# First values drained before the first normalising multiplications, two buffers for the first squares, and k prepared ahead of q

## The chip, the cores and the metric

The kernel runs on one core of one Trainium2 chip. The metric is the device time of one execution in microseconds; the median over several runs counts. Lower is better.

## The reference

A two-layer causal decoder trunk over 512 tokens of width 1024, in float32. Layer 0 has two kinds of attention heads side by side (8 dilated heads "A", 8 sliding-window heads "B" with sinks that share two k/v heads); layer 1 has 16 "forgetting" heads "C". Each layer ends with a squared-ReLU MLP of width 4096.

```python
def forgetting_attention(q, k, v, log_f):         # layer 1; A and B differ in bias and mask
    c = jnp.cumsum(log_f, axis=1)
    s = jnp.einsum("bqhd,bshd->bhqs", qb, k) * scale + c_q - c_k       # causal mask
    return jnp.einsum("bhqs,bshd->bqhd", softmax(s), v)

def reference(x, g_mix, g_mlp, ...):
    for layer in range(2):
        h = rms_norm(x, g_mix[layer])
        # mixer: q, k, v = h @ w_in; q, k = rms_norm per head; attention; @ w_out
        x = x + mixer(h, ...)
        h = rms_norm(x, g_mlp[layer])
        x = x + jnp.square(jax.nn.relu(h @ w_up[layer])) @ w_down[layer]
    return x
```

## The kernel before, in words

Every float32 matrix product is made of three products of rounded parts: an operand x is split into a high part (`whi`, `h[:,0]`, written by ACT or POOL as a cast) and a low part (`wlo`, the remainder, a subtraction on DVE or POOL), and hi·hi + lo·hi + hi·lo are summed in a PSUM bank. So nearly every weight tile needs two elementwise passes before TensorE (PE) may use it.

The work of the five engines is written as one Python program. A scheduling layer then records an order for each engine by its own estimates of durations; instructions passed to `in_order` (while `cnt["start"]` is set) or to `tc.keep_in_program_order` keep the written order among themselves. On the chip each engine works through its recorded order and waits at semaphores. Nearly all transfers are on the queue of SP.

The start of layer 0 runs so:

1. `start` loads the transposed input and the first weights and projects q and k of the first four A heads into the four PSUM banks `pj0` to `pj3` (one for each tile of 128 tokens; L663). Mask tables are built meanwhile on DVE in scratch tiles, of which `f` has the tag `P3` with two buffers.
2. The next projection, `v_a(0)`, makes the first values v into four other banks (L234 to L236, 128x256 matmuls); the one behind it, `kv_b`, makes k and v of the B heads and takes the banks of `v_a(0)` again, each once that is drained.
3. `norm_heads` (L243) copies the q/k banks to the SBUF tiles `qk` (L250), squares them on ACT into a tile with the tag `sq`, of which layer 0 has one buffer (L254), reduces the squares over each head on DVE (L255), takes the inverse root in a chain of small DVE steps (L265 to L268, `rsqrt_small` L130 to L135, in the tile `room`), and multiplies `qk` by it: token tiles 0 and 2 on DVE, 1 and 3 on POOL (L274, `NORM = 'vgvg'`). At the first use the same chain also yields `rcol`, the inverse root mean square of each token (L276).
4. `prep_v` (L310) drains the value banks: for each bank an ACT scaling by `rcol` (L160) and a DVE subtraction (L161), which frees the bank.
5. For each pair of heads, `get` makes the transposed operands. `prep_q` transposes q with four PE transposes (L283, `qkT`), then two ACT casts (L293) and two DVE subtractions (L294). `prep_k` transposes k likewise, then for each of its two heads an ACT scaling (L160), a DVE subtraction (L161) and a transfer on SP that copies k to the other 64 partitions (L306, `K<-K`). Scores (`S`, L341) of a head need its K with that transfer, and its half of Q.

`attend` runs the heads (scores, softmax with P scaled by POOL, DVE or ACT at L363 and L366, transposes of P, L378, values, L398, drained to `yf` at L402), and `run` interleaves them with dense projections (`pj`) or the output projection (`op`).

Of the kernel before, what the change touches and what calls it, by code (L numbers as in the profile page):

```python
# [18 lines left out]
P = 128  # L19
# [3 lines left out]
NT = S // P  # L23
FF = 4096
HD = 64
# [12 lines left out]
NORM = 'vgvg'  # L38
# [31 lines left out]
def trunk(ctx, tc, x, b_sinks, w_out_even, b_forget, w_out_odd, w_up, w_down, xt, gains, w_in_even, w_in_odd, out):  # L70
    nc = tc.nc
# [9 lines left out]
    def bank(tag, name):  # L81
        return ps.tile([P, 512], F32, tag=tag, bufs=BANKS[tag], name=name)
# [114 lines left out]
    def layer_attention(li, hT, w_in, w_out, stats=None):  # L197


        with ExitStack() as c2:  # L200
# [42 lines left out]
            def norm_heads(outs, nh, sq_tag="sq", sq_bufs=1 + li, ms=None):  # L243


                w = nh * HD
                qk = [ap.tile([P, 2, 512], F32, tag="qk", bufs=4, name="qk") for _ in range(2)]
                ss = small.tile([P, NT, 8], F32, tag="ss", name="ss")
                for t in range(NT):
                    nc.scalar.copy(qk[t // 2][:, t % 2, :w], outs[t][:, :w])  # L250
                for t in range(NT):
                    q = qk[t // 2][:, t % 2, :w]
                    sq = ap.tile([P, 512], F32, tag=sq_tag, bufs=sq_bufs, name="sq")
                    nc.scalar.activation(sq[:, :w], q, AF.Square)  # L254
                    nc.vector.reduce_sum(ss[:, t, :nh], sq[:, :w].rearrange("p (h d) -> p h d", d=HD), axis=AX.X)  # L255
                if ms is None:
                    v = small.tile([P, NT, 8], F32, tag="ssv", name="ssv")[:, :, :nh]
                    rs = small.tile([P, NT, 8], F32, tag="rs", name="rs")[:, :, :nh]
                    room = None
                else:  # L260
                    room = ap.tile([P, 512], F32, tag=sq_tag, bufs=sq_bufs, name="room")
                    room = [room[:, i * NT * (nh + 1):(i + 1) * NT * (nh + 1)]
                            .rearrange("p (t h) -> p t h", h=nh + 1) for i in range(5)]
                    v, rs = room[:2]
                    nc.vector.tensor_scalar(v[:, :, nh], ms, 1.0 / D, EPS, op0=OP.mult, op1=OP.add)  # L265
                    nc.vector.tensor_scalar_mul(ecol, v[:, :, nh], EPS)
                for t in range(NT):
                    nc.vector.tensor_scalar(v[:, t, :nh], ss[:, t, :nh], 1.0 / HD, ecol[:, t:t + 1],  # L268
                                            op0=OP.mult, op1=OP.add)
                rsqrt_small(rs, v, room)  # L270
                for t in range(NT):
                    q = qk[t // 2][:, t % 2, :w].rearrange("p (h d) -> p h d", d=HD)
                    eng = nc.gpsimd if NORM[t] == "g" else nc.vector
                    eng.tensor_mul(q, q, rs[:, t, :nh].unsqueeze(2).to_broadcast([P, nh, HD]))  # L274
                if ms is not None:
                    nc.vector.tensor_copy(rcol, rs[:, :, nh])  # L276
                return qk

            def head_T(qk, off):
# [229 lines left out]
            st = {}  # L509

            def v_use(g, i):
                def use(outs):
                    st["v", g] = prep_v(outs, 0, 4, i)
                return use

            def qk_use(key, nh, *sq):
# [8 lines left out]
            if li == 0:  # L525
                def qk_a(g):
                    return project([(g * 768, g * 768 + 512)], qk_use(g, 8))

                def v_a(g):
                    return project([(g * 768 + 512, g * 768 + 768)], v_use(g, 0), PAT_START if g == 0 else PAT_ATT)  # L530

                def att_a(g):
                    def get(p_):
                        qk = st["qk", g]
                        return prep_q(qk, p_ * P), prep_k(qk, 256 + p_ * P, gg[:, 0:1])
                    return attend(get, 256, lambda: st["v", g], lambda j: j, "a", 4 * g, 2, 2 * g)

                def kv_b():
                    def use(outs):
                        st["v", 3] = prep_v(outs, P, 2, 1)  # L540
                        st["k", "b"] = norm_heads(outs, 2)
                    return project([(2048, 2304)], use, PAT_START)

                def att_b():
                    def get(p_):
                        if p_ == 0:
                            st["kb"] = prep_k(st["k", "b"], 0, gg[:, 1:2])
                        k = st["kb"][p_ // 2]
                        return prep_q(st["qk", "b"], p_ * P), [k, k]
                    return attend(get, 0, lambda: st["v", 3], lambda j: j // 4, "b", 0, 4, 4)  # L550

                start(ap, hT, w_in, make_tables(ap, dist, lt, lb), [bank("pA", f"pj{t}") for t in range(NT)], qk_use(0, 8))
                all_of(v_a(0))
                run(att_a(0), 32, chain(kv_b(), project([(1536, 2048)], qk_use("b", 8))), 768, LEADS[0])
                run(att_b(), NB, chain(qk_a(1), v_a(1)), 768, LEADS[1])
                run(chain(att_a(1), last_values()), 38, chain(out_part([0, 1, 4, 5], True),
                                                              out_part([6, 7], False), ahead([2, 3])), 1536, LEADS[2])
                last = [2, 3]
            else:
                def qk_c(g):  # L560
                    return project([(g * 768, g * 768 + 512)], qk_use(g, 8))

                def v_c(g):
                    return project([(g * 768 + 512, g * 768 + 768)], v_use(g, g))

                def vf_c():
                    def use(outs):
                        forget(ap, outs)
                        v_use(0, 0)(outs)
                    return project([(512, 768), (3072, 3088)], use, PAT_START)  # L570

                def att_c(g):
                    def get(p_):
                        qk = st["qk", g]
                        return prep_q(qk, p_ * P), prep_k(qk, 256 + p_ * P, gg[:, 2:3])
                    return attend(get, 256, lambda: st["v", g], lambda j: j, "c", 4 * g, 2, 2 * g)

                g = vf_c()
                for _ in range(STATS):
                    next(g)  # L580
                stats()
                all_of(g)
                all_of(qk_c(0))
                for g in range(3):
                    run(att_c(g), 36, chain(qk_c(g + 1), v_c(g + 1)), 768, LEADS[3 + g])
                run(chain(att_c(3), last_values()), 42, chain(out_part([0, 1, 2, 3], True),
                                                              out_part([4, 5], False), ahead([6, 7])), 1536, LEADS[6])
                last = [6, 7]
# [683 lines left out]
```

## Time and profile before

| what | us |
|---|---|
| median of 3 runs | 1165.46 (1165.13 to 1166.15) |
| profiled execution, its own time | 1166.66 |
| its span | 1164.9 |
| PE busy with matmuls | 1145.0 (98% of the span) |
| DVE busy | 875.5 (75%) |
| ACT busy | 645.9 (55%) |
| POOL busy | 200.3 (17%) |

A line of a timeline reads: start in us, duration in us, engine, source line, operation, output<-input, shape, count; in brackets the idle time of the engine ahead of it and what ended that. PE is TensorE, DVE VectorE, ACT ScalarE, POOL GpSimd, SPq the transfer queue of SP. A line of stretches reads: from:to, length, and for PE, its weight loads, DVE, ACT and POOL the busy time with the number of instructions, then the granted clock of PE, the share of the DMA engines in use, and GB/s. Some matmul records can be missing from a trace.

### The profile page before, as it was taken

How to read it: one execution, taken by the hardware profiler on the slowest of the kernel's cores; microseconds unless marked ns; L12 is line 12 of the kernel's file. 1: busy time of each engine (PE TensorE's matmuls, PEld its weight loads, DVE VectorE, ACT ScalarE, POOL GpSimd, SP SyncE). 2: the span in 40 equal slices, each digit the busy share in tenths (PEclk: the TensorE clock that was granted, in tenths of full speed). 3: DMA queues.
4: the chain of work that ended last, by engine and by line, in shares of the span. 5: the costliest groups of instructions: out<-in, count | busy, mean ns of one | idle time of the engine just before them, and what ended most of it. 6: DMA issues, size and time to landing. Idle time of an engine off the chain costs nothing.

```text
span 1164.9 us, 17364 instructions
## 1 busy us (share of the span) xinstructions
PE 1145.0 (98%) x6228; PEld 980.3 (84%) x6228; DVE 875.5 (75%) x1865; ACT 645.9 (55%) x1342; POOL 200.3 (17%) x292
## 2 busy tenths in 40 slices
PE   9899999999999999999999999999999999999998
PEld 7887887888988988988887888888888888888887
DVE  7787899968967847855646877778858759669676
ACT  7365867565545545444335685656756455465452
POOL 0345434200000000000155445342100000000000
PEclk9899999999999999999999999999999999999999
DMA  8423115242332332333443333343430721623403
GB/s 287 129 75 91 37 37 148 71 127 73 102 116 91 91 109 91 93 118 106 149 122 121 106 86 109 95 133 112 164 104 4 234 90 56 197 73 109 148 34 109
DMA packets 94695, 126.57 MB, mean 109 GB/s; under 512 B 5888, under 2 KB 66304, under 8 KB 94608
## 3 DMA queue, kind: packets, MB, share of 16 engines
q1 hardware_dynamic: 93568, 123.29, 34.7%
q10 hardware_dynamic: 1040, 2.16, 0.5%
q8 instruction: 49, 0.80, 0.3%
q14 instruction: 38, 0.31, 0.1%
HBM read 114.39 MB, written 4.23 MB: 102 GB/s over the span
## 4 chain that ended last, share of the span: by engine, by line
PE 84%; DVE 7%; DMA 3%; ACT 3%; issue 2%; POOL 2%; SPq 0%; POOLq 0%; ACTq 0%; DVEq 0%
PE up L165 10%; PE up L168 10%; PE up L169 10%; PE pj L236 4%; PE pj L234 4%; PE pj L235 4%; PE O L398 3%; PE PT L378 2%; PE op L169 2%; PE op L165 2%; PE op L168 2%; PE Y L1032 2%; PE Y L1030 2%; PE Y L1033 2%; PE S L341 2%
## 5 line engine op out<-in xcount | busy, mean ns | idle before, releaser
L165 PE MATMUL up<-xin,whi 128*128 128x512 f32 x512 | 200.5, 392 | 0.0
L169 PE MATMUL up<-xin,whi 128*128 128x512 f32 x512 | 199.3, 389 | 0.0
L168 PE MATMUL up<-xin,wlo 128*128 128x512 f32 x512 | 199.2, 389 | 0.0
L779 ACT CAST whi<-wraw 128x512 fp32r<-128x512 f32 x228 | 139.2, 619 | 105.1 <-PE up L169 47.4
L780 DVE TENSOR_TENSOR wlo<-wraw,whi 128x512 fp32r<-128x512 f32 x228 | 151.6, 685 | 50.9 <-ACT whi L779 50.8
L169 PEld LDWEIGHTS up<-xin,whi 128*128 128x128 f32 x512 | 96.1, 188 | 20.2
L165 PEld LDWEIGHTS up<-xin,whi 128*128 128x128 f32 x512 | 96.1, 188 | 19.8 <-issue 0.2
L168 PEld LDWEIGHTS up<-xin,wlo 128*128 128x128 f32 x512 | 96.2, 188 | 19.6 <-issue 0.2
L358 ACT ACTIVATE P<-P,negm 128x128 f32<-128x128 f32 (+5 forms) x128 | 69.4, 543 | 46.5 <-DVE negm L355 44.6
L153 POOL TENSOR_SCALAR whi<-wraw 128x512 fp32r<-128x512 f32 x88 | 60.1, 684 | 167.3 <-PE pj L236 123.6
L961 ACT ACTIVATE u<-up 128x512 f32<-128x512 f32 x64 | 38.3, 599 | 90.9 <-PE up L169 90.9
L234 PE MATMUL pj<-whi,hn 128*128 128x512 f32 (+2 forms) x256 | 88.7, 347 | 0.0
L236 PE MATMUL pj<-whi,hn 128*128 128x512 f32 (+2 forms) x256 | 86.9, 340 | 0.0
L235 PE MATMUL pj<-wlo,hn 128*128 128x512 f32 (+2 forms) x256 | 86.8, 339 | 0.0
L800 DVE TENSOR_TENSOR t<-u 128x256 f32<-128x256 f32 x56 | 23.1, 423 | 62.9 <-ACT u L1104 61.1
L156 POOL TENSOR_TENSOR wlo<-wraw,whi 128x512 fp32r<-128x512 f32 x48 | 64.0, 1335 | 21.0 <-ACT whi L151 18.6
L366 POOL TENSOR_SCALAR P<-P,rden 128x256 f32<-128x256 f32 (+2 forms) x96 | 48.9, 512 | 81.5 <-DVE rden L361 76.0
L156 DVE TENSOR_TENSOR wlo<-wraw,whi 128x512 fp32r<-128x512 f32 (+1 forms) x71 | 48.2, 685 | 18.5 <-POOL whi L153 15.0
L390 ACT CAST PT<-PT 128x256 fp32r<-128x256 f32 (+3 forms) x128 | 49.1, 403 | 21.5 <-PE PT L378 20.6
L234 PE MATMUL pj<-whi,h 128*128 128x256 f32 (+1 forms) x160 | 55.4, 346 | 4.6 <-DVE v L161 4.1
L355 DVE CUSTOM_DVE_ANT_0 P<-S,bias 128x128 f32<-128x128 f32 (+1 forms) x96 | 45.7, 485 | 17.8 <-PE S L344 11.9
L779 ACT CAST whi<-mraw 128x512 fp32r<-128x512 f32 x64 | 38.8, 619 | 33.1 <-DVE mraw L890 14.4
(241 smaller groups left out, 3092.1 us busy)
## 6 DMA issues: line engine op xcount, KB each, us to landing
wraw<-in_w_up SPq DMA_DIRECT2D x64, 512.0 KB, 4.3
wraw<-in_w_down SPq DMA_DIRECT2D x56, 512.0 KB, 3.8
wraw<-in_w_in_odd SPq DMA_DIRECT2D x22, 512.0 KB, 3.8
wraw<-in_w_in_even SPq DMA_DIRECT2D x17, 512.0 KB, 4.7
mraw<-in_w_down SPq DMA_DIRECT2D x16, 512.0 KB, 4.7
K<-K SPq DMA_DIRECT2D x26, 256.0 KB, 2.9
bias<-csp SPq DMA_DIRECT2D x16, 256.0 KB, 3.3
wraw<-in_w_out_odd SPq DMA_DIRECT2D x8, 512.0 KB, 3.8
```

What stands on the lines that cost most here:

```text
L153: nc.gpsimd.tensor_scalar(dst_h, src, 1.0, 1.0, op0=OP.mult, op1=OP.mult)
L156: in_order((nc.gpsimd if lo == "pool" else nc.vector).tensor_sub(dst_l, src, dst_h.bitcast(F32)))
L165: m = nc.tensor.matmul(o, wh, xh, start=start, stop=False, skip_group_check=more)
L168: nc.tensor.matmul(o, wl, xh, start=False, stop=False, skip_group_check=more)
L169: nc.tensor.matmul(o, wh, xl, start=False, stop=stop, skip_group_check=more)
L234: nc.tensor.matmul(o, xh, hi[:, :n], start=k == 0, stop=False)
L235: nc.tensor.matmul(o, xh, lo[:, :n], start=False, stop=False)
L236: nc.tensor.matmul(o, xl, hi[:, :n], start=False, stop=k == DC - 1)
L358: nc.scalar.activation(p[:, :ne], p[:, :ne], AF.Exp, scale=-1.0, bias=negm[:, i:i + 1], accum_out=den[:, i:i + 1])
L390: nc.scalar.copy(dst[:, 0], pt[:, :n])
L779: sca(nc.scalar.copy(dst_h, src))
L780: late.append(lambda: vec(nc.vector.tensor_sub(dst_l, src, dst_h.bitcast(F32))))
```

## The change

It has three parts.

- In `norm_heads`, at the first use alone, the multiplications of `qk` are put into a function `normalise` that is kept for later; `rcol` is copied straight behind the inverse root. `v_use` drains the first values first and calls `normalise` behind that, with the written order kept on DVE for both.
- The first `norm_heads` uses the tag `P3` with its two buffers for the squares, instead of the one buffer `sq`.
- For the pairs of A heads (layer 0) and C heads (layer 1), k is prepared ahead of q. B heads are as before.

```diff
-                for t in range(NT):
-                    q = qk[t // 2][:, t % 2, :w].rearrange("p (h d) -> p h d", d=HD)
-                    eng = nc.gpsimd if NORM[t] == "g" else nc.vector
-                    eng.tensor_mul(q, q, rs[:, t, :nh].unsqueeze(2).to_broadcast([P, nh, HD]))
-                if ms is not None:
+                def normalise():
+                    for t in range(NT):
+                        q = qk[t // 2][:, t % 2, :w].rearrange("p (h d) -> p h d", d=HD)
+                        eng = nc.gpsimd if NORM[t] == "g" else nc.vector
+                        m = eng.tensor_mul(q, q, rs[:, t, :nh].unsqueeze(2).to_broadcast([P, nh, HD]))
+                        if eng is nc.vector:
+                            in_order(m)
+
+                if ms is None:
+                    normalise()
+                else:
                     nc.vector.tensor_copy(rcol, rs[:, :, nh])
+                    st["first"] = normalise
                 return qk
...
                 def use(outs):
+                    first = st.pop("first", None)
+                    cnt["start"] = first is not None
                     st["v", g] = prep_v(outs, 0, 4, i)
+                    if first:
+                        first()
+                    cnt["start"] = False
                 return use
...
-                        return prep_q(qk, p_ * P), prep_k(qk, 256 + p_ * P, gg[:, 0:1])
+                        k = prep_k(qk, 256 + p_ * P, gg[:, 0:1])
+                        return prep_q(qk, p_ * P), k
...
-                start(ap, hT, w_in, make_tables(ap, dist, lt, lb), [bank("pA", f"pj{t}") for t in range(NT)], qk_use(0, 8))
+                start(ap, hT, w_in, make_tables(ap, dist, lt, lb), [bank("pA", f"pj{t}") for t in range(NT)], qk_use(0, 8, "P3", 2))
```

The pairs of C heads (`att_c`) change as those of `att_a` do. The recorded order moves in three kinds of places.

DVE at the start, from the last step of the inverse root on (`v0` the first values, `pj0` to `pj3` their banks, `wlo_832` the low part of a weight whose `whi_831` POOL makes). Before:

```order
L135 SCALAR_TENSOR_TENSOR room_382<-room_382 128x36
L274 TENSOR_TENSOR qk_363<-qk_363,room_382 128x512
L274 TENSOR_TENSOR qk_364<-qk_364,room_382 128x512
L276 COPY rcol_95<-room_382 128x4
L161 SCALAR_TENSOR_TENSOR v0_103<-pj0_409,rcol_95,v0_103 128x4x64
L161 SCALAR_TENSOR_TENSOR v0_103<-pj1_410,rcol_95,v0_103 128x4x64
L161 SCALAR_TENSOR_TENSOR v0_103<-pj2_411,rcol_95,v0_103 128x4x64
L156 TENSOR_TENSOR wlo_832<-wraw_825,whi_831 128x512
L161 SCALAR_TENSOR_TENSOR v0_103<-pj3_412,rcol_95,v0_103 128x4x64
```

And on the same engine at the same place with the change:

```order
L135 SCALAR_TENSOR_TENSOR room_382<-room_382 128x36
L282 COPY rcol_95<-room_382 128x4
L161 SCALAR_TENSOR_TENSOR v0_103<-pj0_405,rcol_95,v0_103 128x4x64
L161 SCALAR_TENSOR_TENSOR v0_103<-pj1_406,rcol_95,v0_103 128x4x64
L161 SCALAR_TENSOR_TENSOR v0_103<-pj2_407,rcol_95,v0_103 128x4x64
L156 TENSOR_TENSOR wlo_832<-wraw_825,whi_831 128x512
L161 SCALAR_TENSOR_TENSOR v0_103<-pj3_408,rcol_95,v0_103 128x4x64
L275 TENSOR_TENSOR qk_363<-qk_363,room_382 128x512
L275 TENSOR_TENSOR qk_364<-qk_364,room_382 128x512
```

The two multiplications went behind the four drains; `wlo_832` stays between the third and the fourth drain. POOL's order at this place does not move: whi and wlo of one weight, its two multiplications of `qk`, then `whi_831`, another whi and a wlo.

PE at the start, where `kv_b`'s projection (`pj0_537` to `pj3_540`, its first products with `h0_0`) has taken three banks. Before:

```order
L236 MATMUL pj2_539<-whi_543,h0_0_180 128x256
L283 MATMUL qkT_563<-ident_72,qk_363 128x128
L234 MATMUL pj3_540<-whi_543,h0_0_180 128x256
L235 MATMUL pj3_540<-wlo_544,h0_0_180 128x256
L236 MATMUL pj3_540<-whi_543,h0_0_180 128x256
L283 MATMUL qkT_563<-ident_72,qk_363 128x128
L283 MATMUL qkT_563<-ident_72,qk_364 128x128 x2
L283 MATMUL qkT_573<-ident_72,qk_363 128x128 x2
L283 MATMUL qkT_573<-ident_72,qk_364 128x128 x2
```

The same place of PE with the change:

```order
L236 MATMUL pj2_539<-whi_543,h0_0_180 128x256
L234 MATMUL pj0_537<-whi_543,h0_1_200 128x256
L234 MATMUL pj3_540<-whi_543,h0_0_180 128x256
L235 MATMUL pj3_540<-wlo_544,h0_0_180 128x256
L236 MATMUL pj3_540<-whi_543,h0_0_180 128x256
L235 MATMUL pj0_537<-wlo_544,h0_1_200 128x256
L236 MATMUL pj0_537<-whi_543,h0_1_200 128x256
L290 MATMUL qkT_563<-ident_72,qk_363 128x128 x2
L290 MATMUL qkT_576<-ident_72,qk_363 128x128 x2
L234 MATMUL pj1_538<-whi_543,h0_1_200 128x256
L290 MATMUL qkT_563<-ident_72,qk_364 128x128 x2
L290 MATMUL qkT_576<-ident_72,qk_364 128x128 x2
```

All eight transposes now stand behind the fourth bank's products (`qkT_563` is q's before and k's with the change), first those of `qk_363` (token tiles 0 and 1), then those of `qk_364`.

PE in layer 1, at the first scores of the first pair of C heads (`hn` is layer 1's normalised input). Before:

```order
L236 MATMUL pj2_6731<-whi_6831,hn_6283 128x512
L234 MATMUL pj3_6732<-whi_6831,hn_6283 128x512
L235 MATMUL pj3_6732<-wlo_6832,hn_6283 128x512
L341 MATMUL S_6852<-K_6816,Q_6806 128x256
L342 MATMUL S_6852<-K_6816,Q_6806 128x256
```

The same scores with the change:

```order
L236 MATMUL pj1_6730<-whi_6831,hn_6283 128x512
L234 MATMUL pj2_6731<-whi_6831,hn_6283 128x512
L235 MATMUL pj2_6731<-wlo_6832,hn_6283 128x512
L348 MATMUL S_6852<-K_6806,Q_6819 128x256
L349 MATMUL S_6852<-K_6806,Q_6819 128x256
```

The scores stand three matmuls earlier in the projection. At the other pairs of layer 1 they move by none (second pair), six (fourth), two (fifth, seventh) or three. In layer 0's output part, scores and transposes of the first pair of the last A heads move by one to eight matmuls, and on POOL one scaling of P (128x384) goes ahead of a `whi` that it stood behind. On SP's queue, two loads of weights in layer 1 change places with a bias transfer. On ACT and DVE, each pair has its k step ahead of its q step.

More of the change, by code (lines that the diff above doesn't have):

```diff
@@ L574, in get @@
                         qk = st["qk", g]
-                        return prep_q(qk, p_ * P), prep_k(qk, 256 + p_ * P, gg[:, 2:3])
+                        k = prep_k(qk, 256 + p_ * P, gg[:, 2:3])
+                        return prep_q(qk, p_ * P), k
                     return attend(get, 256, lambda: st["v", g], lambda j: j, "c", 4 * g, 2, 2 * g)
```

## The prediction

> **What bounds the kernel now.** I read the page first (its span and the row of granted clock by slices), then the waits of PE, because a kernel whose PE is busy 98% of the span can gain only where PE stands or runs slow, then the timelines around each long wait. The profiled execution took 1166.66 us around its span; the median of the runs shown is 1165.46, and what I sum against the span I take off the median.
>
> ```profile
> span 1164.9 us, 17364 instructions
> PEclk9899999999999999999999999999999999999999
> PE pj L234 <- DVE v L161: 4.1, 2, 3.5
> PE S L341 <- DMA K<-K: 1.9, 3, 1.1
> PE PT L378 <- POOL P L366: 0.8, 1, 0.8
> ```
>
> The last three rows are PE's waits that this change touches (us in total, times, longest). The first is the largest, and the second slice of the clock row, 29 to 58 us, is the only one below 9 tenths; both are the same place. PE there, then its stretches (length, PE busy with its matmuls, other engines, granted clock):
>
> ```profile
> 41.47 0.28 PE L236 MATMUL pj<-whi,h 128*128 128x256 f32 x1
> 45.25 0.39 PE L234 MATMUL pj<-whi,h 128*128 128x256 f32 x1 [3.50 <-DVE v L161]
> 47.63 0.58 PE L234 MATMUL pj<-whi,h 128*128 128x256 f32 x1 [0.62 <-DVE v L161]
> ...
> 46.40:49.78 3.38, 2.76 (x14) 2.37 (x13) 1.17 (x2) 0.47 (x1) 0.23 (x1) 0.50 0.35 105
> 49.78:53.13 3.35, 3.35 (x18) 3.35 (x17) 2.12 (x3) 2.06 (x4) 0.35 (x1) 0.50 0.23 73
> 53.13:56.40 3.27, 3.27 (x29) 3.27 (x29) 1.45 (x2) 0.00 (x0) 0.76 (x2) 0.99 0.59 110
> 106.00:109.40 3.40, 1.71 (x8) 1.00 (x8) 2.09 (x2) 0.00 (x0) 3.40 (x3) 1.00 0.85 227
> ```
>
> The first values' projection ends at 41.75. The next projection needs a bank that DVE has not drained: idle 3.50, and 0.62 for the fourth bank, 4.12 in all. A good microsecond after PE resumes the clock falls to 0.50 for two stretches, together 6.73 us, of which 6.11 with work. The second has 18 matmuls in 3.35 us, the one behind it 29 in 3.27: a rate of 0.61, so 6.11 x 0.39 = 2.4 us are lost. The place costs 4.1 + 2.4 = 6.5 us, of which a change at the drain can win a part. The last row is for later: 3.4 us with PE busy for half of it kept the clock.
>
> **Why the drain is late.** DVE and POOL, from the squares to the drain:
>
> ```profile
> 32.41 0.69 DVE L255 TENSOR_REDUCE ss<-sq 128x8 f32<-128x512 f32 x1 [1.07 <-ACT sq L254]
> 35.18 0.69 DVE L255 TENSOR_REDUCE ss<-sq 128x8 f32<-128x512 f32 x1
> 36.11 0.61 DVE L266 TENSOR_SCALAR ecol<-room 128x4 f32<-128x4 f32 x1
> 36.76 1.74 DVE L268 TENSOR_SCALAR room<-ss,ecol 128x8 f32<-128x8 f32 x4
> 38.53 0.18 DVE L130 TENSOR_SCALAR room<-room 128x36 int32<-128x36 int32 x1
> 41.04 2.14 DVE L274 TENSOR_TENSOR qk<-qk,room 128x512 f32<-128x512 f32 x2
> 43.11 1.00 DVE L276 COPY rcol<-room 128x4 f32<-128x4 f32 x1
> 44.71 1.27 DVE L161 SCALAR_TENSOR_TENSOR v<-pj,rcol,v 128x256 fp32r<-128x256 f32 x3 [0.60 <-ACT v L160]
> 45.90 1.28 DVE L156 TENSOR_TENSOR wlo<-wraw,whi 128x512 fp32r<-128x512 f32 x1
> 47.10 0.47 DVE L161 SCALAR_TENSOR_TENSOR v<-pj,rcol,v 128x256 fp32r<-128x256 f32 x1
> ...
> 36.08 0.62 POOL L153 TENSOR_SCALAR whi<-wraw 128x512 fp32r<-128x512 f32 x1 [22.77 <-DVE room L265]
> 36.78 1.29 POOL L156 TENSOR_TENSOR wlo<-wraw,whi 128x512 fp32r<-128x512 f32 x1
> 41.14 2.95 POOL L274 TENSOR_TENSOR qk<-qk,room 128x512 f32<-128x512 f32 x2 [3.07 <-issue]
> 44.06 1.20 POOL L153 TENSOR_SCALAR whi<-wraw 128x512 fp32r<-128x512 f32 x2
> 45.34 1.29 POOL L156 TENSOR_TENSOR wlo<-wraw,whi 128x512 fp32r<-128x512 f32 x1
> ...
> 73.52 0.62 DVE L135 SCALAR_TENSOR_TENSOR rs<-rsq 128x8 f32<-128x8 f32 x1
> L274 POOL TENSOR_TENSOR qk<-qk,rs x2: 1045/1268/1490, 645.5 to 646.5; 128x512 f32<-128x512 f32 x2
> ```
>
> DVE operations that read only SBUF end when POOL's do: ecol (0.61) with POOL's whi at 36.70, the rcol copy (1.00) at 44.11 with POOL's second multiplication at 44.09, wlo (1.28) half a microsecond after POOL's wlo. The drains (L161, 0.4 each) read PSUM and do not. POOL's multiplication itself takes 1.05 where no such DVE operation runs (645.5) and 1.49 beside one.
>
> **The change, part by part.**
>
> Two buffers for squares. The second square need not wait for the first reduction, so the idle 1.07 and two tenths before each later reduction go: the fourth reduction ends near 34.1 instead of 35.87. But POOL's whi and wlo (36.08 to 38.07) wait for PE and stay, and now the eleven small steps of the inverse root (38.53 to 41.04: 0.23 each) run into them; 73.52 shows such a step beside a POOL whi: 0.62. I let two to four steps pass before or between and the others follow 38.07: seven to nine, so the root ends at 39.7 to 40.2, take 39.9 instead of 41.04. Bounds: 38.4 if nothing collides, 41.04 if all do. No added work.
>
> Values ahead of the multiplications. The rcol copy follows the root directly, 39.9 to 40.1 (0.2 like the steps around it, since POOL has only begun); in the row it ended at 44.11. So the first three drains shift by 4.0: PE finds its first three banks free at 41.75 and does not wait. The fourth bank does: DVE's order keeps a wlo between third and fourth drain, and that needs a whi that POOL makes behind its two multiplications: 40.1 + 2 x 1.05 = 42.2, + 0.62 = 42.8; DVE's wlo then stands behind POOL's second whi (to 43.4), ends at 44.0, the drain at 44.45, PE goes on at 44.5. PE has then done nine matmuls and one of the next chunk (41.75 + 10 x 0.12 = 42.95): idle 1.55. With POOL at 1.49 per multiplication it is 2.4; without the collision about 0.6.
>
> The multiplications behind them. DVE's first now starts at 44.45, stands behind POOL's wlo (to 45.3) and ends at 45.9. PE does five matmuls (to 45.1), then wants its transpose: idle 0.85 (0 to 1.6). The second ends at 46.5, by when PE is through four transposes and a matmul: nothing. Idle here: 1.55 + 0.85 = 2.4 against 4.12.
>
> The clock. Between 42.95 and 45.95 PE works 0.6 us, less than in the quoted 106.00 row that kept its clock, more evenly than the 3.50 us gap that lost it; no row lies between. Bounds: no half-clock stretch (0 lost) and two as now (2.4 to 2.6). I take one of 3.4 us, 3.4 x 0.39 = 1.3: the low stretch is as long as one of those two, and the work that kept the second going slow (transposes, 0.62 idle) now lies ahead of it. Loss 2.4 + 1.3 = 3.7 against 6.5: **gain 2.8** (1.3 to 4.1). The Trainium skill, "TensorE: Matmul & The Clock Gate", section "Why this matters for your kernels", says that one window of idle returns the clock to half and to leave no gap over about 3 us. The 3.50 us gap here agrees; by that rule two gaps of 1.55 and 0.85 would keep the clock, which is the first rival below.
>
> k first. In layer 1, PE stands for K's transfer (the copy to the other half of the partitions):
>
> ```profile
> 626.25 0.36 PE L341 MATMUL S<-K,Q 128*128 128x256 f32 x1 [1.15 <-DMA K<-K]
> 621.97 0.74 DVE L161 SCALAR_TENSOR_TENSOR K<-qkT,gg,K 64x512 fp32r<-64x512 f32 x1
> 622.74 2.01 SPq L306 DMA_DIRECT2D K<-K  x2
> 647.81 0.36 PE L341 MATMUL S<-K,Q 128*128 128x256 f32 x1 [0.55 <-DMA K<-K]
> 685.81 0.28 PE L341 MATMUL S<-K,Q 128*128 128x256 f32 x1
> 682.60 2.02 SPq L306 DMA_DIRECT2D K<-K  x2
> 735.38 0.62 POOL L153 TENSOR_SCALAR whi<-wraw 128x512 fp32r<-128x512 f32 x1 [2.96 <-PE pj L236]
> 737.62 0.27 PE L341 MATMUL S<-K,Q 128*128 128x256 f32 x1
> 734.50 2.03 SPq L306 DMA_DIRECT2D K<-K  x2
> ```
>
> K's step on DVE moves ahead of one Q step, so SP issues 0.7 earlier; Q's lateness of 0.75 hides under the transfer's 3.1 to 3.5 (734.50 to 737.62; 622.74 to 626.25). But the recorded order takes that gain in advance: PE's scores also stand earlier among the projection's matmuls (0.23 each). First pair: three matmuls, 0.69, so its wait of 1.15 stays. Second pair: none, 0.55 goes. Fourth pair (685.81): six, 1.4 against 0.7, a new wait of 0.3 to 0.65. The third to eighth otherwise move two or three, about even; the third recorded wait, 0.2, goes. Sum **gain 0.3** (-0.6 to 1.4). On SP's queue two of layer 1's loads of weights now stand behind a bias transfer. POOL's whi waits there for PE (735.38), not for a load, so I cost this at nothing; with that cover gone, PE would stand for some tenths at each of the two loads.
>
> Layer 0's output part is recorded in another order too. One wait and its cause:
>
> ```profile
> 180.22 0.33 PE L378 MATMUL PT<-ident,P 128*128 128x128 f32 x1 [0.85 <-POOL P L366]
> 178.46 1.14 POOL L153 TENSOR_SCALAR whi<-wraw 128x512 fp32r<-128x512 f32 x1 [1.34 <-DMA wraw<-in_w_out_even]
> ```
>
> P's multiplication now stands ahead of that whi, so 0.85 goes; but a score bank is wanted sooner behind yf, which may cost 0.3 to 0.8. **Gain 0.2** (-0.9 to 0.9).
>
> Sum: 2.8 + 0.3 + 0.2 = 3.3, that is 1165.46 - 3.3 = about **1162.2 us**.
>
> **Rivals.**
> The clock never falls: no gap reaches the length of the one that lost it, and the row at 106.00 kept 1.00 with 1.7 us idle. Gain 4.1 + 0.5: 1160.9. Against it: only 0.6 us of work in 3 us. 25%.
> POOL stays the gate: the root does not end earlier (41.04) or POOL takes 1.49, the fourth drain comes at 45.4 or later, and two slow stretches remain: idle 3.3 + 2.6 = 5.9 against 6.5; with the rest 1.1: 1164.4. For it: POOL's two operations at 36 us do not move. 18%.
> K's transfer leaves no earlier (DVE reaches K when its other work lets it) while PE reaches the scores earlier: 22 matmuls over seven pairs, 22 x 0.23 = 5.1, nearly no slack in the rows above. Against 2.8 + 0.2: slower by 2.1, 1167.5. It decides from 3.0 us of new waits; for it, the first pair, where DVE comes from other work; against it, its order, K first at each pair. 6%.
> The change does little: the wait only moves to the fourth bank and the transposes, idle 4 us with two stretches; with 0.3 elsewhere: 1165. 8%.
> My forecast has 43%.
>
> **Numbers.** A measurement tells 0.2% (2.3 us) from no change. The forecast's case spreads from 1161.6 to 1163.6, mostly beyond 1163.1: three quarters faster. With the first rival and a little of the second: faster 0.60; within 0.2%: 0.33; slower 0.07. Range 1160.5 to 1165.2: it leaves out the slower rival and the tails.
>
> **What the profile will show.** PE's wait for v near 41.75 gone, one of some 1.5 us for the fourth bank near 43 and one below 1 us at a transpose; the rcol copy at 0.2 us near 40, right behind the root; one half-clock stretch. K waits in layer 1 near 1.6 us, one of them at the fourth pair. The forecast is wrong if the root still ends at 41 us, if the clock shows none or two slow stretches, or if the new waits in layer 1 exceed 1 us each.

## The result: slower by 0.25%, where 0.28% faster was forecast

The changed kernel took 1168.74 us (median of 16 executions, 1164.42 to 1172.29) against 1165.43 for the kernel before on the same chip (16 executions, 1164.64 to 1167.04). The ratio is 1.0025, with a 95% interval of 1.0017 to 1.0034. Not only is the middle higher: the executions spread over 8 us instead of 2.4. In the experiments further down, one execution of f3 (6491 us) and one of j2 (2926 us) took several times as long as the others and are left out of their numbers.

The profiled execution took 1170.03 us. Its page, the span and the granted clock by slices:

```profile
span 1168.2 us, 17366 instructions
PEclk9999999999999999999999999999999999999999
```

The low second slice of before is gone. PE's waits in the same execution (us in total, times, longest):

```profile
PE S L348 <- DMA K<-K: 8.4, 6, 2.8
PE qkT L290 <- DVE qk L275: 1.2, 2, 0.7
PE pj L234 <- DVE v L161: 1.0, 1, 1.0
```

The wait for the first values fell from 4.1 to 1.0 us. The wait of the scores for K's transfer rose from 1.9 to 8.4 us. The change won at one place and lost more at others.

**The start.** The timelines of DVE, POOL and PE there, as shown of before in the prediction:

```profile
38.90 0.20 DVE L135 SCALAR_TENSOR_TENSOR room<-room 128x36 f32<-128x36 f32 x1
39.13 0.17 DVE L282 COPY rcol<-room 128x4 f32<-128x4 f32 x1
39.90 1.27 DVE L161 SCALAR_TENSOR_TENSOR v<-pj,rcol,v 128x256 fp32r<-128x256 f32 x3 [0.60 <-ACT v L160]
41.90 1.09 DVE L156 TENSOR_TENSOR wlo<-wraw,whi 128x512 fp32r<-128x512 f32 x1 [0.73 <-POOL whi L153]
42.91 0.47 DVE L161 SCALAR_TENSOR_TENSOR v<-pj,rcol,v 128x256 fp32r<-128x256 f32 x1
...
39.23 2.05 POOL L275 TENSOR_TENSOR qk<-qk,room 128x512 f32<-128x512 f32 x2 [1.57 <-issue]
...
43.44 0.39 PE L234 MATMUL pj<-whi,h 128*128 128x256 f32 x1 [0.95 <-DVE v L161]
44.81 0.63 PE L290 MATMUL qkT<-ident,qk 128*128 128x128 f32 x4 [0.52 <-DVE qk L275]
```

The root ends at 39.10, the rcol copy takes 0.17 us right behind it, POOL's two multiplications take 2.05, and PE stands only for the fourth bank (0.95) and for the first transposes (0.52). And the clock stays up in this execution. The stretches (length, PE, weight loads, DVE, ACT, POOL busy, then the granted clock):

```profile
41.75:45.15 3.40, 1.93 (x15) 1.55 (x14) 3.25 (x4) 0.05 (x1) 2.28 (x3) 1.00 0.24 57
45.15:48.55 3.40, 3.40 (x31) 3.40 (x30) 2.07 (x4) 2.36 (x4) 0.62 (x1) 1.00 0.29 107
```

**K's transfers.** The two longest waits of the scores, at the first pair of A heads beside layer 0's output part and at the first pair of layer 1, with SP's queue ahead of each:

```profile
179.42 1.46 SPq L184 DMA_DIRECT2D wraw<-in_w_out_even  x2
182.31 2.60 SPq L313 DMA_DIRECT2D K<-K  x2
189.43 0.36 PE L348 MATMUL S<-K,Q 128*128 128x256 f32 x1 [2.65 <-DMA K<-K]
...
609.66 8.11 SPq L184 DMA_DIRECT2D wraw<-in_w_in_odd  x2
618.07 1.97 SPq L313 DMA_DIRECT2D K<-K  x2
623.36 0.36 PE L348 MATMUL S<-K,Q 128*128 128x256 f32 x1 [2.78 <-DMA K<-K]
```

A row with x2 runs from the first issue to the end of the second. So a load's issue ended at 617.77, 0.3 us ahead of the transfer of K (609.66 + 8.11 against 618.07). Before, it was 1.1 us (613.50 + 8.12, against 622.74 in the prediction's row):

```profile
613.50 8.12 SPq L184 DMA_DIRECT2D wraw<-in_w_in_odd  x2
```

The landings of all 26 transfers of K, from the view of that tile, of before and then of after:

```profile
DMA to landing us min/median/max: 2.8/2.9/4.9
```

```profile
DMA to landing us min/median/max: 2.8/3.7/7.0
```

Both long waits then cost once more, by the clock. Behind the wait at 189 us it is 0.50 from 190.8 to 194.2; behind the one at 623 us it is 0.50 from 624.3 to 627.6, which shows as 0.66 and 0.84 in the two rows that share it:

```profile
190.80:194.20 3.40, 3.40 (x13) 2.71 (x12) 2.98 (x11) 3.40 (x13) 1.99 (x4) 0.50 0.57 192
...
619.80:623.20 3.40, 0.77 (x4) 0.31 (x2) 1.17 (x2) 0.88 (x1) 0.00 (x0) 1.00 1.03 266
623.20:626.60 3.40, 3.24 (x13) 2.54 (x14) 1.60 (x9) 1.80 (x6) 0.79 (x2) 0.66 0.43 125
626.60:630.00 3.40, 3.40 (x17) 2.49 (x16) 1.58 (x8) 1.41 (x5) 2.48 (x4) 0.84 0.07 24
```

The spread goes with the clock. The two executions with a mean clock of 1.000 took 1165.2 us on average, the five with 0.996 or less 1170.3. A stretch of 3.4 us at half clock lowers the mean by 3.4 x 0.5 / 1168 = 0.0015, so 0.004 is two to three stretches. At the rate of 0.61 that the prediction read off, each costs about 1.3 us, so they make an estimated 3.5 of the 5 us; that the waits ahead of them were longer too in those executions is likely and not shown.

### The profile page after: what moved, and what is told of

The parts are those of the page before. It is cut to its first block, busy times and chain, and to the rows that moved or that the text cites. A ratio compares the mean times of both kernels' runs of the same rounds, so it can differ in the third digit from the quotient of the medians.

```text
span 1168.2 us, 17366 instructions
## 1 busy us (share of the span) xinstructions
PE 1146.4 (98%) x6228; PEld 980.3 (84%) x6228; DVE 875.6 (75%) x1865; ACT 646.1 (55%) x1342; POOL 199.2 (17%) x292
## 4 chain that ended last, share of the span: by engine, by line
PE 82%; DVE 7%; DMA 4%; ACT 3%; POOL 2%; issue 2%; SPq 0%; DVEq 0%; ACTq 0%; POOLq 0%
PE up L165 10%; PE up L169 10%; PE up L168 10%; PE pj L236 4%; PE pj L234 4%; PE pj L235 4%; PE O L405 3%; DMA K<-K 2%; PE PT L385 2%; PE Y L1047 2%; PE Y L1044 2%; PE Y L1046 2%; PE op L169 2%; PE op L168 2%; PE op L165 2%
```

## The experiments

Theory A: the loss is k first, and within it transfers of K that land late because they leave close behind a load of weights. Theory B: the loss is k first, but by the recorded order, in which the scores stand earlier. (In the expectations of the first four runs A stands for both.) Theory C: the start's gain moved the kernel by 6 us against its loads, and that made the collisions.

| run | start parts | k first in | else | us (executions) | ratio to before, 95% |
|---|---|---|---|---|---|
| e1_start_only | yes | – | | 1161.36 (7) | 0.9967 (0.9956–0.9977) |
| e2_kfirst_only | no | both layers | | 1171.17 (5) | 1.0059 (1.0046–1.0073) |
| e3_kfirst_l0 | yes | layer 0 | | 1162.08 (11) | 0.9975 (0.9966–0.9984) |
| e4_kfirst_l1 | yes | layer 1 | | 1167.31 (11) | 1.0018 (1.0009–1.0027) |
| g1_values_first | values alone | – | | 1163.12 (11) | 0.9981 (0.9973–0.9990) |
| g2_two_buffers | buffers alone | – | | 1164.06 (11) | 0.9994 (0.9985–1.0002) |
| h1_half_kfirst_l1 | yes | layer 1 | half q, k loads | 1164.60 (12) | 0.9999 (0.9990–1.0007) |
| h2_half_qfirst | yes | – | half q, k loads | 1160.44 (5) | 0.9961 (0.9949–0.9973) |
| h3_allhalf_kfirst | yes | layer 1 | all loads half | 1162.40 (9) | 0.9976 (0.9967–0.9985) |
| h4_allhalf_qfirst | yes | – | all loads half | 1159.70 (5) | 0.9950 (0.9938–0.9962) |
| i1_clear_pairs | yes | two pairs | | 1161.53 (8) | 0.9970 (0.9960–0.9980) |
| f3_k_on_act | yes | layer 1 | K by ACT's queue | 1167.63 (11) | 1.0020 (1.0011–1.0029) |
| j1_scores_held | yes | layer 1 | scores as q first | 1161.81 (6) | 0.9968 (0.9957–0.9980) |
| j2_held_loads_behind | yes | layer 1 | both | 1159.21 to 1162.88 (4) | 0.9961 (0.9947–0.9975) |
| j3_loads_behind | yes | layer 1 | loads behind K | 1164.84 (11) | 0.9995 (0.9986–1.0004) |
| j4_qfirst_loads_behind | yes | – | loads behind K | 1163.13 (8) | 0.9979 (0.9969–0.9989) |

(Half loads: layer 1's attention weights, with a part of them left out. e1 to e4 ran on one chip, g1 to h2 on a second, h3 to f3 on a third, the j runs on a fourth; the kernel before stood between 1165.03 and 1165.44 beside them.)

### Which part loses

Start alone, from the changed kernel:

```diff
-                        k = prep_k(qk, 256 + p_ * P, gg[:, 0:1])
-                        return prep_q(qk, p_ * P), k
+                        return prep_q(qk, p_ * P), prep_k(qk, 256 + p_ * P, gg[:, 0:1])
```

and the same in `att_c`. For e3 only `att_c` has q first again, for e4 only `att_a`; e2 has the kernel before with the lines above turned round.

> The two start parts of the change, with q ahead of k as before. Theory A (k first is the loss): by 100 us the changed kernel's trace stood 6.2 us ahead of before (the first wait of a transpose after that is at 100.56 instead of 106.78), and nothing behind the start moves here, so 1165.4 - 6 = 1159.4 us, between 1158.5 and 1160.5, with PE's wait for K's transfers at 1 to 2 us in all as before. Rival C (standing 6 us earlier against the loads of weights is what makes K's transfers collide, whatever the order of q and k): those waits stay near 8 us and the time is 1166 to 1169.

> K ahead of q in both layers, the start as before. Theory A: slower by what the changed kernel lost behind its start, 3.3 + 6.2 = 9.5 us, so 1172 to 1177, with 7 to 10 us of PE's waits for K's transfers and a wide spread from run to run. Rival C: the transfers don't collide without the start's shift, 1164 to 1167. The forecast's step, k first a gain of 0.3 (-0.6 to 1.4), would give 1164 to 1166 too.

> The changed kernel with k first in layer 0 alone (layer 1 has q first again). Theory A puts one wait of 2.65 us, at 189 us, and about 1 us of small ones behind layer 0's part of k first: some 3.5 us over the start alone, 1162 to 1164. If layer 1 holds all of the loss, 1159 to 1160.

> The changed kernel with k first in layer 1 alone. Theory A: waits of 2.78, 0.97, 0.73 us and two small ones, 5.7 us in all against 1.9 before, and a stretch at half clock behind the 2.78 (3.3 us long, 1.3 lost): some 5 us over the start alone, 1163.5 to 1166. If layer 0 holds all of the loss, 1159 to 1160. The two parts of k first should add up to the changed kernel: start alone + layer 0's loss + layer 1's loss = 1168.7 within 1.5.

The start alone is 4.0 us faster than before (expected: 6, read off the profiled execution of before, which was itself 1.2 us slower than its median). K first alone is 5.8 slower (1171.17, just below its expected 1172 to 1177). Theory C falls: without the start's shift k first loses most of what it loses with it (1168.74 - 1161.36 = 7.4). Layer 1's part costs 6.0. Layer 0's part costs 0.7, which is not clear of the spread (e3 from 1160.61 to 1164.79, e1 from 1159.67 to 1162.18): its wait at 190 us was 1.65 us, a wait for P of 0.85 and one for negm of 1.1 went away in exchange. The medians add up: 1161.36 + 0.7 + 6.0 = 1168.1, against 1168.74 measured.

PE's waits in e1 and then in e4:

```profile
PE S L348 <- DMA K<-K: 1.8, 3, 1.1
PE O L405 <- DVE PT L398: 0.4, 2, 0.3
```

```profile
PE S L348 <- DMA K<-K: 5.1, 5, 2.1
PE O L405 <- DVE PT L398: 1.3, 4, 0.6
```

These two profiled executions are 5.7 us apart (1161.36 and 1167.04). The waits for K make 3.3 of it, those for P's transposes 0.9, and one stretch at half clock (621.0 to 624.4 us in e4, none in e1) about 1.3: 5.5 in all.

The first pair of layer 1, q first (e1) and then k first (e4): SP's queue, PE's first scores.

```profile
608.10 8.12 SPq L184 DMA_DIRECT2D wraw<-in_w_in_odd  x2
617.34 2.01 SPq L313 DMA_DIRECT2D K<-K  x2
620.72 0.35 PE L348 MATMUL S<-K,Q 128*128 128x256 f32 x1 [1.06 <-DMA K<-K]
```

```profile
607.83 8.12 SPq L184 DMA_DIRECT2D wraw<-in_w_in_odd  x2
616.23 1.97 SPq L313 DMA_DIRECT2D K<-K  x2
620.82 0.42 PE L348 MATMUL S<-K,Q 128*128 128x256 f32 x1 [2.08 <-DMA K<-K]
```

Against the load ahead of it (ending at 616.22 and at 615.95) the transfer leaves 1.12 and 0.28 us later: 0.84 earlier with k first (0.7 was forecast). But the scores can start 4.5 us behind the load with q first and 4.87 with k first: the transfer that left earlier did not land earlier. The load shows why: issued at 615.85 in e1 and at 615.58 in e4, it lands 3.7 and 4.0 us later, near 619.6 both times, and K's transfer lands about 1.1 us behind it in both runs. PE, by the recorded order, was there 0.65 us sooner, counted from the load (619.66 and 618.74). So the wait doubled. At the second pair no scores moved, and the wait still rose from 0.62 to 1.09: the transfer left 0.39 instead of 1.33 us behind its load and took 4.9 instead of 3.5 us to land.

### The two parts of the start

g1 is e1 with `qk_use(0, 8)`, g2 is the kernel before with `qk_use(0, 8, "P3", 2)`.

> Only the first values ahead of the normalising multiplications: one buffer for squares, q ahead of k. If this part carries the start's 4.0 us, 1161 to 1162, PE's clock at 1.00 behind the first drains and the wait for v below 1.5 us in all. If the two buffers are needed for the clock to stay up (the root then ends at 41 instead of 40 us and the fourth drain a microsecond later), a stretch at half clock stays and the time is 1163 to 1164.

> Only the two buffers for squares; multiplications ahead of the values and q ahead of k as before. The inverse root ends up to 1.1 us earlier and the wait of 3.5 us for the first drained bank falls by as much, to 2.4 to 3.3. With the clock falling as before: 1164.3 to 1165.3. If a gap of 2.4 no longer makes it fall: 1162.

Values first gains 1.9 us. Its profiled execution has a stretch at low clock (46.9 to 50.2 us, cut in two by these rows); PE waits ahead of it for 0.62, 1.47 and 0.52 us:

```profile
44.80:48.20 3.40, 2.59 (x15) 2.42 (x16) 2.12 (x3) 0.31 (x1) 0.97 (x1) 0.80 0.51 154
48.20:51.60 3.40, 3.40 (x23) 3.40 (x22) 2.95 (x5) 2.11 (x4) 0.62 (x1) 0.70 0.17 36
```

Two buffers alone gain 1.0 (not clear of no gain), and there the executions part by the clock: the two with a mean clock of 1.000 took 1162.6 us on average, the two with 0.996 took 1165.1. Together they gain 4.0, more than 1.9 + 1.0. The clock has a part in that: four of seven executions of e1 kept 1.000, three of eleven of g1, two of eleven of g2. It is not all: among the executions at 1.000, e1 stands at 1160.7 us on average, g1 at 1162.4 and g2 at 1162.6, and the start's waits in the profiles are 1.2 us in e1 and 2.6 to 2.7 in the other two. How much of the excess is beyond the spread was not settled.

### Late transfers or early scores

Halving the bytes of the loads, as h1 and h2 do it for the q and k loads; h3 and h4 do the same for all loads of layer 1's attention weights (the scores stand in h1 where they stand in e4; in h3 a few stand one to seven matmuls earlier still):

```diff
+            if half:
+                src, n = src[:P], P
             nc.sync.dma_start(raw[:, k:k + n // P, c:c + m], ...)
...
+            k1 = 0 if half else k
-            hi, lo = parts(raw[:, k:min(k + m, kw)], ...)
+            hi, lo = parts(raw[:, k1:min(k1 + m, kw)], ...)
```

> The start parts with k first in layer 1 alone, and each load of q and k weights of layer 1 brings only its first half (256 KB instead of 512; the second half's products use the first half's weights again, so a part of the weights is left out). PE's recorded order is that of the run with full loads. Theory A (K's transfer lands late because it shares the DMA engines with the load that SP issued 0.3 to 0.8 us ahead of it): K's transfers at 616 and 640 us land in 2.8 to 3.5 us instead of 3.9 to 4.9, the waits for them fall from 5.1 to 1.5 to 2.5 us, and the time is 0 to 2.5 us over the q-first kernel with half loads. Theory B (the scores stand earlier in PE's order, and that alone makes the loss): landings don't matter, waits stay at 4 to 5, and the time stays 4 to 6 us over it.

> The control: the start parts, q ahead of k everywhere, the same half loads of layer 1 (a part of the weights left out). Theories A and B alike: K's transfers leave 1.1 to 1.3 us or more behind a load and land in 2.8 to 3.2, so of the 1.8 us of waits at most 1 goes: 1160.3 to 1161.4, against 1161.4 with full loads. More than that would mean that the loads themselves hold something up in layer 1.

> The start parts with k first in layer 1 alone, and now every load of weights for layer 1's attention (q, k, v and the output projection) brings half of its bytes; the other half's products use the first half's weights again, so a part of the weights is left out. Where only the q and k loads were halved, the loss of k first fell from 6.0 to 4.2 us, and the one transfer behind a halved load (at 616 us) landed in 3.1 instead of 4.2, while those behind full loads (637, 761, 785 us) still took 3.7 to 4.3. Theory A (the transfer shares the DMA engines with the load ahead of it): now all land in 2.8 to 3.5, and the loss against the control falls to 1 to 2.5 us, which is what the scores' earlier places leave. Theory B (the order alone): the loss stays at 4.

> The control: q first, the same halves of layer 1's attention weights left out. K's transfers land in 2.8 to 3.0 everywhere in layer 1; 1159.8 to 1161 us, as with only the q and k loads halved (1160.44).

The loss of k first in layer 1 fell from 6.0 to 4.2 (1164.60 - 1160.44) with the q and k loads halved, which by its expectation speaks for theory B (4 to 6); but most of the late transfers still stood behind full loads there. It fell to 2.7 (1162.40 - 1159.70) with all halved, slightly above what theory A allowed (1 to 2.5) and below theory B's 4. The first pair with all loads halved:

```profile
615.72 0.33 SPq L189 DMA_DIRECT2D wraw<-in_w_in_odd  x1
616.38 1.98 SPq L319 DMA_DIRECT2D K<-K  x2
619.87 0.35 PE L354 MATMUL S<-K,Q 128*128 128x256 f32 x1 [1.02 <-DMA K<-K]
```

The same 0.33 us behind a load, but a load of 256 KB: the wait is 1.02 instead of 2.08. So the bytes of the load ahead delay the transfer. One transfer does not fit: in h4, at 660 us, one that left 0.5 us behind a half load took 4.8 us, and the trace does not show why. Is it SP's queue or the DMA engines? f3 issues K's transfers from ACT:

```diff
-                    nc.sync.dma_start(k[r2].bitcast(F32), k[r].bitcast(F32))
+                    nc.scalar.dma_start(k[r2].bitcast(F32), k[r].bitcast(F32))
```

> The start parts with k first in layer 1 alone, and all of K's transfers issued from ACT's queue instead of SP's. The recorded order moves elsewhere too, so the total is a poor witness; the landings are the question. If the transfer is late because it stands behind the load in SP's queue, it lands in 2.8 to 3.0 us however near a load is, and the time falls to 1160 to 1163. If what they share is the DMA engines, a transfer that leaves within 0.7 us of a load still takes 3.5 to 5, and the time is 1164 to 1169, with ACT's issues (some 0.5 us each, 26 of them) in its way.

SP's loads (the issue of the first ended at 616.77) and ACT's transfer at the first pair, and how long that transfer took to land:

```profile
616.40 3.16 SPq L184 DMA_DIRECT2D wraw<-in_w_in_odd  x2
617.06 0.47 ACTq L313 DMA_DIRECT2D K<-K  x1
```

```profile
DMA to landing us min/median/max: 5.0/5.0/5.0
```

From another queue it is as late (5.0). The other transfers of layer 1 that left 0.39 to 0.43 us behind a load took 4.2 to 4.7, and the total stayed at 1167.6: the engines behind the queues are shared, and another queue does not help. The Trainium skill, "DMA: Bandwidth & Descriptors", section "Issuing engines are not separate DMA queues", says that transfers started by different engines end up on the same 16 DMA engines and interleave there; this trace agrees, with its 5.0 us.

Then the pairs whose transfers leave clear of loads:

```diff
+                        if p_ == 1 and g in (1, 2):
+                            k = prep_k(qk, 256 + p_ * P, gg[:, 2:3])
+                            return prep_q(qk, p_ * P), k
+                        return prep_q(qk, p_ * P), prep_k(qk, 256 + p_ * P, gg[:, 2:3])
```

> The start parts, and k first at only two pairs of layer 1, the second pair of the second and of the third group, whose transfers leave 1.7 and 4.2 us behind a load and landed in 2.8 to 2.9 us with k first too. Full loads. Their scores move three matmuls (0.7 us) earlier each. Theory A: K leaves 0.7 earlier and lands 0.7 earlier, so no loss: within 0.5 of the start alone, 1160.9 to 1161.9. Theory B (scores earlier, K not): 2 x 0.7 slower, 1162.5 to 1163.

1161.53, 0.2 from the start alone: where the transfer lands in 2.8 to 2.9 us, three matmuls earlier cost nothing. But nor did they gain anything. Up to here theory A held mostly. The last four runs show that it is a part of the story. j1 pins the first scores of layer 1's heads to the places that they have with q first; j3 puts six loads behind K's transfers; j2 does both, j4 has the loads so with q first:

```diff
+    for m, n in zip(first_s, (1031, 1032, 1125, ...)):                       # j1, j2
+        tc.add_manual_dep(m.ins, dense[n - 1].ins.name, ...)
+    for n, c in [(20, 11), (23, 13), (25, 15), (29, 19), (30, 19), (33, 23)]:  # j2, j3, j4
+        tc.add_manual_dep(loads[n].ins, copies[c].ins.name, ...)
```

> The start parts with k first in layer 1 alone, and the first scores of each of layer 1's 16 heads pinned in PE's order behind the very matmul behind which they stand with q first (they move by none against the start alone; K's steps and transfers stay ahead of q's). If the scores' earlier places make most of the 6.0 us that k first loses in layer 1, the time falls to 1161.4 to 1163. If the transfers that leave 0.3 to 0.8 us behind a load make most of it (they land no earlier for leaving earlier, 3.7 to 5 us instead of 2.9 to 3.2), it stays at 1163.5 to 1166. My own split, from the halved loads: 2.7 of the 6.0 remained with all loads halved, so 1167.3 - 2.7 = 1164.6.

> As the run with held scores, and the six loads of layer 1's weights that SP issues within 0.9 us ahead of a transfer of K are put behind that pair's two transfers in SP's order. Full loads, nothing left out. If collision and order are the whole of the loss, K now lands in 2.8 to 3 us, 0.7 us before the scores want it, and the time is that of the start alone or a little less, 1160.3 to 1161.5. If the loads, now 2 to 3 us later, are wanted sooner than that, PE waits for whi or wlo instead, 1163 or more.

> K first in layer 1 with the start parts, the same six loads behind the transfers, and the scores where the scheduler puts them (two to seven matmuls earlier). By the halved loads, where a loss of 2.7 us remained with every transfer landing in 2.8 to 3.4: 1161.4 + 2.7 = 1164, between 1162.5 and 1165, with K waits of 1 to 2 us.

> The start parts with q first everywhere, and the same six loads behind K's transfers: can the best version be bettered without k first? The waits for K of 1.1 and 0.6 us at 620 and 642 us follow landings of 3.1 to 3.5 us behind loads issued 1.1 to 1.3 us earlier; at 2.8 they fall by 0.3 to 0.7 each. 1160.4 to 1161.4, against 1161.36 for the start alone; 1163 or more if the later loads are missed.

With the scores held, 5.5 of the 6.0 us are gone (1161.81), though the transfers still leave 0.29 us behind the load and land late. My own estimate, 1164.6, was wrong. Its profiled execution was the slowest of the six (1164.22), and shows what is left:

```profile
617.24 1.97 SPq L314 DMA_DIRECT2D K<-K  x2
622.38 0.36 PE L349 MATMUL S<-K,Q 128*128 128x256 f32 x1 [1.96 <-DMA K<-K]
```

PE reaches the scores at 620.42, 3.18 us behind the transfer's issue, where it was 2.51 in e4; of the late landings only this one (5.0) still costs more than 1 us. Of the six executions four kept a clock of 1.000 (1160.8 to 1162.62), against two of eleven in e4.

The other way round, the order alone: with the loads behind the transfers, which all land in 2.8 to 3.1 us, the early scores cost 1164.84 - 1163.13 = 1.7 us. The loads' new places cost 1.4 to 1.8 by themselves (j4 against e1, by the ratios to before and by the times); in j4's profile PE waits 1.91 us at the last pair for a transfer that landed in 2.8 us but left late. In j3's profiled execution the profile puts no wait above 0.4 us down to K (1 to 2 us were expected); what replaced it are waits of 1.2 for negm, 0.56 for a PT and 1.3 for the accumulator, that is, the softmax chain and the drains are late next. The last of these is K's as much: its transfer, issued at 785.76, landed at 788.6, 0.1 us before the scores started. And the wait for negm is at the second pair, whose scores stand seven matmuls earlier in j3 than in e1 but did not move in e4, so 1.7 may be too much for e4's order. j2 is inconclusive beside e1: its four executions spread over 3.7 us.

So layer 1's 6.0 us divide roughly so: late transfers without early scores 0.45 (j1), early scores without late transfers 1.7 (2.7 by h3), and the rest, 3 to 4 us, only where both meet, a stretch at low clock in most executions among it. Each of these is a difference of medians of five to eleven executions that spread over as much as 5 us, and is uncertain by a microsecond or more. How much of that rest is the clock I can only bound: between executions of e4 with a mean clock of 1.000 (1165.4) and its median it is 1.9 us.

## Why the prediction was wrong

- **What bounds the kernel, and the wait for the first values**: the places were right, the sizes too large. The wait of 3.50 us went, the wait for the fourth bank came where it was forecast (0.95 against 1.55), the one at the transposes too (0.52 against 0.85). The root ended at 39.1, ahead of the forecast 39.7 to 40.2, because six of the eleven small steps were left when POOL's pair ended, where seven to nine were counted, and that pair ended at 37.7 instead of 38.1 (38.4 was the bound). The 45.3 for POOL's wlo is not what the prediction's own terms give (42.2 + 1.2 + 1.3 = 44.7); with 44.7 the wait at the transposes would have been about 0.2.
- **The clock at the start**: the term was mis-sized. I took one stretch at half clock; in the changed kernel and in e1's profile there is none at the start, which was the first rival. Start alone: 4.0 us, against 2.8 (1.3 to 4.1) forecast and 4.1 for the rival. The row at 106 us, from which the prediction argued that such work keeps the clock, was luck: the same place, with the same gaps of PE (0.65, 0.51 and 0.54 or 0.55 us), lost the clock in the profiles of e2, e3 and j1. In e3:

```profile
104.10:107.50 3.40, 3.40 (x12) 2.73 (x10) 1.64 (x3) 1.16 (x2) 1.50 (x2) 0.50 0.00 0
```

- **k first, a gain of 0.3 (-0.6 to 1.4)**: this step failed, and its range with it. It measured as a loss of 6.0 in layer 1. The working took the transfer's duration as 3.1 to 3.5 us however early it leaves, so that 0.7 us earlier out would be 0.7 earlier in. In its place the runs showed that at the first pair it leaves 0.84 earlier and lands no earlier: it shares the DMA engines with the load ahead and lands about 1.1 us behind it with either order. The price was there to be read in the trace of before, where three transfers that leave 0.4 to 0.5 us behind a load landed in 4.7 to 4.9 us. The first of them, and its landing:

```profile
54.15 0.38 SPq L184 DMA_DIRECT2D wraw<-in_w_in_even  x1
54.94 0.47 SPq L306 DMA_DIRECT2D K<-K  x1
```

```profile
DMA to landing us min/median/max: 4.8/4.8/4.8
```

  I had looked at SP's queue only for which transfers change places in it, not for the distances between them, and took the landing from the rows where it was short.
- **"The recorded order takes that gain in advance"**: right, and it was the main point. The forecast of a new wait at the fourth pair (685.81) did not come true: that transfer left 1.7 us behind a load and landed in 2.9 us. The waits came at the first, second, seventh and eighth pairs.
- **The third rival** (K no earlier, scores earlier; 1167.5, decided from 3.0 us of new waits) is nearest to what happened: 6.5 us of new waits (8.4 - 1.9), 1168.74 us. I gave it 6%, and argued against it from DVE's order. K did leave earlier; it was the landing that stood still, which e1 and e4 show at the first pair; j1 (scores held: loss gone) and h1 to h4 (loads halved: loss more than halved) show both sides of the cost.
- **Layer 0's output part, gain 0.2 (-0.9 to 0.9)**: e3 measured a loss of 0.7, in the range, but by waits that the working did not count. The wait for P at 180 us went as forecast; a wait for K of 2.65 us (1.65 in e3) at 189 us took its place, behind two loads.
- **Range and spread**: the forecast had no place for the executions spreading apart. A wait near 2 us in front of scores may or may not cost a stretch at low clock.

The best version of those that leave no weights out is the start alone, 1161.36 us, 0.33% faster than before (0.23 to 0.44); i1, j1 and j2 cannot be told from it.

## What to carry to other kernels

Where a transfer is started earlier, look at what stands ahead of it on all queues at its new time: here it left 0.8 us earlier and landed no earlier behind a load of 512 KB. If the scheduler counts on the earlier landing and moves the consumer up, the consumer waits; hold the consumer where it stood, or leave the order alone. Time the parts of a change apart: here one part gained 4.0 us and the other hid it.

## What the runs showed of the hardware

- A transfer of K (256 KB, SBUF to SBUF) landed in 2.8 to 3.1 us when it left 1.7 us or more behind the end of the issue of a single 512 KB load, mostly in 2.8 to 3.5 at 1.1 to 1.5 us, in 3.0 to 4.3 at 0.7 to 0.9, and in 3.7 to 5.2 at 0.3 to 0.5 (by the first transfer of a pair, both of the pair counted, in the traces of before, after, e1, e4 and j1). Behind two loads issued together it took 5.8 and 7.0 (182 us). Landings of 3.5 to 4.3 us at the last pair (788 to 793 us, after and e4) had the last load 4.3 us ahead, but that load itself took 8.3 to 8.4 us to land and was still on its way. What fits all of these is the load's landing: in these traces the first transfer behind a load issued less than 1.4 us ahead landed 0.4 to 1.6 us after that load had landed, and those of the last pair 0.6 us after (the first of the pair).
- Where the granted clock fell inside these profiles, it fell to 0.50 for about 3.4 us (6.8 in before). It did so behind gaps of PE of 1.68, 1.84 and 2.71 (f3), 1.96 (j1), 2.08 (e4), 2.13 (e2 at 626 us), 2.65 and 2.78 us (both in after). It did not behind 1.83 (g2), 1.91 (j4) and 2.11 us (e2 at 194 us), nor behind 0.95 and 0.52 us close together at the start. The three short gaps at 101 to 109 us, at most 0.65 us each and nearly the same in all kernels, were followed by such a stretch in e2, e3 and j1 and by none in before, after, e1 and e4. So the length of a gap alone does not decide. The Trainium skill, "TensorE: Matmul & The Clock Gate", section "Why this matters for your kernels", advises to leave no gap over about 3 us; here gaps of 1.7 to 2.1 us, and at one place shorter ones close together, cost a stretch in some executions, so the measurement sets a lower limit than the page. What decides between such cases was not tried.
